# Two MLPs' up-projection in another order, sums of weight blocks given out later, a recurrence's head started later

## The chip, the cores and the metric

One of the eight cores of a Trainium2 chip runs the program. TensorE (PE) multiplies, VectorE (DVE), ScalarE (ACT) and GpSimd (POOL) do the elementwise work, SyncE (SP) issues the loads. The metric is the device time of one execution in microseconds, as the median of several runs.

## The reference

The program is one inference step of a small trunk: a layer with a gated linear recurrence and an MLP, then a layer with dilated windowed attention and an MLP. There are 1024 positions of a prompt and 32 of samples, 1056 columns in all; the width is 1024, the MLPs' hidden width 4096, all in fp32. What the change touches most is the MLP:

```python
def _sqrelu_mlp(x, w_up, w_down):
    return jnp.square(jax.nn.relu(x @ w_up)) @ w_down
...
x = x + _sqrelu_mlp(_rmsnorm(x, mlp_norm[layer]), mlp_w_up[layer], mlp_w_down[layer]).astype(x.dtype)
```

The change also shifts the start of the recurrence's first head. There the state of each of eight heads, 128 x 128, follows S_t = diag(f_t) S_(t-1) + k_t v_t^T, o_t = S_t^T q_t, in chunks.

## The kernel before

Activations lie transposed, features on the partitions and columns along the row. Each fp32 product is three passes of TensorE over a split into a high and a low part: high by high, high by low, low by high (lines L190 to L192 in `mm3`, L986 to L988 in `mmx`). So everything that is multiplied is first split: ScalarE copies the high part, and POOL or VectorE subtracts it from the value to get the low one. For weights that is `_prep` (L131 for `whi` on ScalarE, L132 for `wlo` on POOL, after a load into `wraw`, of which there are few buffers); for hidden values it is `split` in `mlp` (L768 and L769).

The columns fall into three chunks, 384 and 384 and 288. On the first two chunks the MLP uses a scheme of seven products in place of eight for 2 x 2 blocks. It needs sums of blocks of the weights, `wsum` (L159 to L161 on VectorE, L162 on POOL), which are split like weights into `whix` and `wlox`, and combinations of the right operands (L773 and L780 in `combine`). The third chunk is multiplied plainly (`third`, `alone`).

Hidden rows come in eight groups in each MLP. `unit(g, i)`, two for a group, makes 2 x 128 hidden rows: the first half of the inner dimension K by the seven products, whose intermediate sums go through tiles `t` (copies L813 on ScalarE, adds L817 on VectorE); then the rest of K by four plain blocks, `plain(e, c)`, for row block e and chunk c, each of which also takes the relu, the scale and the square and splits the result: (0,0) is entry 0 of the hidden operand `hb`, (1,0) entry 1, (1,1), the corner, entry 2; entries 3 to 6 are combinations. Of chunk 0 POOL makes the low part, otherwise VectorE. L817 and L838 or L834 are the evacuation on VectorE, L839 the square on ScalarE. Of the third chunk the two halves of K are `third(e, 0)` and `third(e, 1)`.

After the two units of a group (but the last), `down` turns the group's hidden rows into four pairs of outputs and adds them to the residual `xr` (L1008; L216 for the third chunk). Its products use `hb` by index: first 0, second 1, third 5, fourth 4, then 6, 3 and 2. Here "down 0" is the first pair of a group, "dn0" to "dn3" are the weights of the four pairs, and "uA" and "uB" those of the units.

A scheduler sets each engine's order from the order in which the code issues the work, with `high_priority` sections moved ahead. `wahead` and `wtake` give out the loads, splits and sums of the next weights; `tick` drives generators that run beside the main work, the late norm (`norm_late`, L311 the scale, L325 the sum over partitions on TensorE) and the recurrence's heads (`gla`; L519 its transposes of `vT`) among them.

Of the kernel before, what the change touches and what calls it, by code (L numbers as in the profile page):

```python
# [28 lines left out]
PW = 384  # L29
# [17 lines left out]
class Kern:  # L47
    def __init__(self, nc, tc, aps, ctx):
        self.nc, self.tc, self.a, self.ctx = nc, tc, aps, ctx
        self.const = ctx.enter_context(tc.tile_pool(name="const", bufs=1))  # L50
        self.op = [self.const.tile([P, KD, NT], F32R, name=n) for n in ("opH", "opL")]
        self.chunks = CHUNKS
        self.wp = ctx.enter_context(tc.tile_pool(name="wp", bufs=2))
        self.pp = ctx.enter_context(tc.tile_pool(name="pp", bufs=4, space=PSUM))
        self.pg = ctx.enter_context(tc.tile_pool(name="pg", bufs=4, space=PSUM))
        self.wx = None
        self.wt = {}
        self.wi = 0
        self.wq = self.weight_order()
        self.queue, self.lanes = deque(), []  # L60
        self.merged = 0
        self.every, self.ticks = 0, 0
        self.rawx = False
        self.twos = False
        self.fine = False
# [59 lines left out]
    def _prep(self, i):  # L125
# [8 lines left out]
        with self.tc.high_priority(offset=400 if i > 1 else 0):  # L134
# [15 lines left out]
            self.wt[i] = (hi, lo)  # L150
        if two:
            with self.tc.high_priority(offset=20):

# [10 lines left out]
                pair(sh, sl, 4, u)  # L164
                self.wt[i] = (hi, lo), (sh, sl)

# [166 lines left out]
    def phase_a(self):  # L333
# [144 lines left out]
        self.open_scales()  # L478
        self.lanes.append(self.norm_late(G_M0, ops, NEED, hp=100))
        next(self.lanes[-1])  # L480
# [103 lines left out]
    def gla(self, h, b, kt, q, vT, og):  # L584

        nc, gp, a = self.nc, self.gp, self.a
        vt = gp.tile([P, 8, P], F32, name="vt8", bufs=1)
        for i in range(2):
# [163 lines left out]
    def mlp(self, layer, ops, after=None):  # L752
# [46 lines left out]
        def unit(g, i):  # L799
# [98 lines left out]
            if not first:  # L898
                W1 = self.wtake()
                self.wahead(self.wi)  # L900
                order = [lambda: third(0, 1), lambda: third(1, 1)]
                rest = [lambda: plain(1, 0, "c"), lambda: plain(0, 0, "a")]
                for f in rest[::-1] if last else order + rest:
                    yield
                    f()
                yield
                bank[1, 1] = self.bank()[:, :PW]
                plain(1, 1, "b", True)
                yield
            else:  # L910
# [8 lines left out]
                split(h[2], x)  # L919
            plain(0, 1)  # L920
            if not last:
                h = rows()
                combine(t, lambda k, v: split(h[k], v))
            if last:
                for f in order:
                    yield
                    f()

# [6 lines left out]
        for g in range(NG):  # L935
# [4 lines left out]
            B = [hb[i][1] for i in range(2)]  # L940
            W = self.wtake()
            self.wahead(self.wi)
            for i in range(2):
                self.alone(0, i, W, hs)
                self.tick()
            for p in range(4):
                if p < 3:
                    nxt = []

                    def fill(i):  # L950
                        if not nxt:
                            nxt.append(self.wtake())
                        self.alone(2 * p + 2, i, nxt[0], hs)
                        self.tick()
                else:
                    u = unit(g + 1, 0)
                    fill = lambda i: next(u)
                self.down(2 * p, W, B, fill)
                self.tick()
                if p < 3:  # L960
                    W = nxt[0]
                    self.wahead(self.wi)
        self.sctx.close()
        w = [self.wnext() for _ in range(4)]
# [79 lines left out]
    def phase_c(self, ops):  # L1044
# [56 lines left out]
        self.open_scales()  # L1101
        self.lanes.append(self.norm_late(G_M1, ops, NEED))
        next(self.lanes[-1])
# [558 lines left out]
```

## Time and profile before

| | |
|---|---|
| median of 3 runs | 3006.82 us (3006.81 to 3012.26) |
| profiled execution | 3012.01 us, its span 3010.2 us |
| TensorE busy | 2856.8 us, 95% of the span |
| VectorE busy | 1832.2 us, 61% |
| ScalarE busy | 1426.9 us, 47% |
| GpSimd busy | 1374.9 us, 46% |
| mean granted clock of TensorE | 0.988 of full speed |

The engine's waits and the timeline of one group are the places to read: what each of TensorE's pauses waited for, how often it comes, and what the engine named was doing just then. Windows show the clock that was granted in a stretch: the share that is missing from it, times the stretch's length, is the time lost.

### The profile page before, as it was taken

Reading aid. Unit: us, or ns where it says so; the run is one execution under the profiler, and the core shown is the slowest. Engines: PE = TensorE matmul, PEld = TensorE weight load, DVE = VectorE, ACT = ScalarE, POOL = GpSimd, SP = SyncE. Lnnn points to the kernel's source line nnn. Section 1 sums busy time; section 2 is a strip of 40 time slices with the busy share of each in tenths; the row PEclk is TensorE's granted clock in tenths of the full one; section 3 lists DMA queues with packets and bytes.
Section 4 is the critical chain, followed back from the end, with each engine's and each line's share of the span. In section 5 each row is a group of like instructions: output and inputs, shape, how many; then the busy total and the mean of one; then the engine's idle time right before and its main releaser. Section 6 shows DMA issues by size and latency. Waiting matters only on the chain.

```text
span 3010.2 us, 47500 instructions
## 1 busy us (share of the span) xinstructions
PE 2856.8 (95%) x17952; PEld 2725.9 (91%) x17952; DVE 1832.2 (61%) x3661; ACT 1426.9 (47%) x3233; POOL 1374.9 (46%) x1159
## 2 busy tenths in 40 slices
PE   6999999899999999999999999999998999999999
PEld 5999899899999999999889889889888999999999
DVE  8777777956555545554755555565686555655553
ACT  6677667745333333333445545555555333333332
POOL 5454444534455445454554454343115545445452
PEclk9999999999999999999999999999999999999999
DMA  3111210221111111112212234332631111111112
GB/s 114 37 32 35 73 39 30 86 100 35 43 50 43 43 50 43 50 43 76 92 48 71 75 103 116 125 113 77 218 119 46 47 49 44 47 45 46 46 50 86
DMA packets 131957, 201.91 MB, mean 67 GB/s; under 512 B 26320, under 2 KB 65872, under 8 KB 129680
## 3 DMA queue, kind: packets, MB, share of 16 engines
q1 hardware_dynamic: 131728, 198.88, 21.1%
q8 instruction: 141, 2.31, 0.3%
q14 instruction: 88, 0.72, 0.1%
HBM read 164.04 MB, written 34.80 MB: 66 GB/s over the span
## 4 chain that ended last, share of the span: by engine, by line
PE 54%; DVE 12%; POOL 9%; DMA 7%; issue 5%; ACT 4%; POOLq 0%; DVEq 0%; SPq 0%; ACTq 0%
PE pj L190 7%; PE pj L191 6%; PE pj L192 6%; POOL wlo L132 6%; PE pj L986 6%; PE pj L987 6%; PE pj L988 6%; DMA wraw<-w_dn 4%; PE g L986 3%; PE g L987 3%; PE g L988 3%; PE g L1333 2%; DMA wraw<-w_uA 2%; PE g L1305 2%; DVE tmp L838 1%
## 5 line engine op out<-in xcount | busy, mean ns | idle before, releaser
L132 POOL TENSOR_TENSOR wlo<-wraw,whi 128x512 fp32r<-128x512 f32 x404 | 535.5, 1345 | 715.8 <-ACT whi L131 684.4
L190 PE MATMUL pj<-opH,whi 128*128 128x352 f32 (+2 forms) x1872 | 637.8, 341 | 4.9 <-ACT opH L237 3.5
L191 PE MATMUL pj<-opL,whi 128*128 128x352 f32 (+2 forms) x1872 | 611.7, 327 | 1.5 <-POOL opL L238 1.2
L192 PE MATMUL pj<-opH,wlo 128*128 128x352 f32 (+2 forms) x1872 | 609.8, 326 | 2.7 <-POOL wlo L132 2.7
L131 ACT ACTIVATE whi<-wraw 128x512 fp32r<-128x512 f32 x404 | 232.7, 621 | 360.8 <-PE pj L987 248.6
L190 PEld LDWEIGHTS pj<-opH,whi 128*128 128x128 f32 x1872 | 357.1, 191 | 23.5 <-issue 12.8
L191 PEld LDWEIGHTS pj<-opL,whi 128*128 128x128 f32 x1872 | 358.2, 191 | 11.6 <-issue 5.7
L192 PEld LDWEIGHTS pj<-opH,wlo 128*128 128x128 f32 x1872 | 356.3, 190 | 6.5 <-POOL wlo L132 3.5
L1008 DVE TENSOR_TENSOR xr<-xr,pj 128x384 f32<-128x384 f32 x336 | 181.4, 549 | 134.2 <-PE pj L988 133.1
L132 POOL TENSOR_TENSOR wlox<-wsum,whix 128x512 fp32r<-128x512 f32 x176 | 231.5, 1336 | 44.4 <-ACT whix L131 44.4
L162 POOL TENSOR_TENSOR wsum<-wraw,wsum 128x256 f32<-128x256 f32 x88 | 68.5, 778 | 358.3 <-DVE wsum L160 239.0
L131 ACT ACTIVATE whix<-wsum 128x512 fp32r<-128x512 f32 x176 | 106.6, 628 | 190.9 <-PE pj L987 69.7
L986 PE MATMUL g<-opH,whi 128*128 128x288 f32 (+1 forms) x640 | 195.1, 305 | 0.0
L987 PE MATMUL g<-opL,whi 128*128 128x288 f32 (+1 forms) x640 | 194.6, 304 | 0.0
L988 PE MATMUL g<-opH,wlo 128*128 128x288 f32 (+1 forms) x640 | 194.1, 303 | 0.0
L986 PE MATMUL pj<-opH,whi 128*128 128x384 f32 x512 | 174.9, 342 | 3.4 <-ACT whi L131 3.4
L988 PE MATMUL pj<-opH,wlo 128*128 128x384 f32 x512 | 173.8, 339 | 1.5 <-POOL wlo L132 1.5
L987 PE MATMUL pj<-opL,whi 128*128 128x384 f32 x512 | 173.7, 339 | 0.0
L544 POOL TENSOR_TENSOR lv<-b 128x512 f32<-128x512 f32 x112 | 125.1, 1128 | 104.3 <-PE g L645 56.7
L159 DVE TENSOR_TENSOR wsum<-wraw 128x256 f32<-128x256 f32 x88 | 46.2, 525 | 142.1 <-DMA wraw<-w_dn 73.7
L986 PEld LDWEIGHTS g<-opH,whi 128*128 128x128 f32 x640 | 120.7, 189 | 0.0
L988 PEld LDWEIGHTS g<-opH,wlo 128*128 128x128 f32 x640 | 120.5, 188 | 0.0
(431 smaller groups left out, 7648.2 us busy)
## 6 DMA issues: line engine op xcount, KB each, us to landing
wraw<-w_dn SPq DMA_DIRECT2D x128, 256.0 KB, 2.9
wraw<-w_in SPq DMA_DIRECT2D x64, 256.0 KB, 2.8
wraw<-w_uA SPq DMA_DIRECT2D x64, 256.0 KB, 2.9
wraw<-w_uB SPq DMA_DIRECT2D x64, 256.0 KB, 2.9
wraw<-w_q SPq DMA_DIRECT2D x48, 256.0 KB, 3.0
ub<-us SPq DMA_DIRECT2D x32, 256.0 KB, 2.2
cc<-ck SPq DMA_DIRECT2D x8, 1024.0 KB, 4.9
cc<-cv SPq DMA_DIRECT2D x8, 1024.0 KB, 5.1
```

What stands on the lines that cost most here:

```text
L131: nc.scalar.activation(hi[:, j:j + 4, :], raw, AF.Copy)
L132: nc.gpsimd.tensor_tensor(lo[:, j:j + 4, :], raw, hi[:, j:j + 4, :].bitcast(F32), op=ALU.subtract)
L162: nc.gpsimd.tensor_tensor(u[:, 2:], a12, t[:, 2:], op=ALU.subtract)
L190: nc.tensor.matmul(ps, wh[:, kw, :], xh[:, kx, :], start=(i == 0), stop=False)
L191: nc.tensor.matmul(ps, wh[:, kw, :], xl[:, kx, :], start=False, stop=False)
L192: nc.tensor.matmul(ps, wl[:, kw, :], xh[:, kx, :], start=False, stop=(i == len(ks) - 1))
L544: nc.gpsimd.tensor_tensor(r(lv), r(b), r(b)[:, :, h - 1:h].to_broadcast([P, 256 // h, 2 * h]), op=ALU.subtract)
L986: nc.tensor.matmul(ps, wh[:, kw, :], xh, start=start and i == 0, stop=False, skip_group_check=True)
L987: nc.tensor.matmul(ps, wh[:, kw, :], xl, start=False, stop=False, skip_group_check=True)
L988: nc.tensor.matmul(ps, wl[:, kw, :], xh, start=False, stop=stop and i == len(items) - 1, skip_group_check=True)
L1008: self.nc.vector.tensor_tensor(x(i, c), x(i, c), ps, op=ALU.add)
L1305: nc.tensor.matmul(out[r], qs[r][:, j * P:(j + 1) * P], k, start=True, stop=True)
```

## The change

Four parts. (a) In the groups with a `down`, the sums of the next weights are not given out with the load and the split but are kept in `sumq` and given out by `flush`, in the fill of the next pair of outputs. (b) In all units but the first and those of the last group, the rest of K goes in the order (0,0), corner, (0,1), (1,0), after the third chunk's two; it was (1,0), (0,0), corner, (0,1). (c) The first head of the recurrence yields two steps before it starts. (d) `norm_late` takes three more steps ahead of the last of its gaps, in both MLPs. No instruction is added or taken away.

```diff
@@ _prep
         if two:
+            box = []
+            self.wt[i] = (hi, lo), box
+
+            def sums():
+                box.extend(self.sums(raws, pair))
+            if self.late:
+                self.sumq.append(sums)
+            else:
+                sums()
+
+    def flush(self):
+        while self.sumq:
+            self.sumq.pop()()
+
+    def sums(self, raws, pair):
+        nc = self.nc
+        if True:
             with self.tc.high_priority(offset=20):
...
-                self.wt[i] = (hi, lo), (sh, sl)
+                return sh, sl
@@ the norms ahead of the MLPs
-        self.lanes.append(self.norm_late(G_M0, ops, NEED, hp=100))
+        self.lanes.append(self.norm_late(G_M0, ops, NEED, (3, 3, 5), 100))
...
-        self.lanes.append(self.norm_late(G_M1, ops, NEED))
+        self.lanes.append(self.norm_late(G_M1, ops, NEED, (3, 3, 5)))
@@ gla
+        if h == 0:
+
+            yield from (None,) * 2
@@ unit
+                def corner():
+                    bank[1, 1] = self.bank()[:, :PW]
+                    plain(1, 1, "b", True)
                 order = [lambda: third(0, 1), lambda: third(1, 1)]
-                rest = [lambda: plain(1, 0, "c"), lambda: plain(0, 0, "a")]
-                for f in rest[::-1] if last else order + rest:
+                rest = [lambda: plain(0, 0, "a"), corner, lambda: plain(0, 1), lambda: plain(1, 0, "c")]
+                if last:
+                    rest = [rest[0], rest[3], rest[1], rest[2]]
+                for f in rest + order if last else order + rest:
                     yield
                     f()
-                yield
-                bank[1, 1] = self.bank()[:, :PW]
-                plain(1, 1, "b", True)
-                yield
...
-            plain(0, 1)
+                plain(0, 1)
@@ mlp
             W = self.wtake()
+            self.late = True
             self.wahead(self.wi)
...
                         self.alone(2 * p + 2, i, nxt[0], hs)
+                        self.flush()
                         self.tick()
                 else:
                     u = unit(g + 1, 0)
-                    fill = lambda i: next(u)
+
+                    def fill(i):
+                        next(u)
+                        self.flush()
...
+            self.late = False
```

In the kernel after, lines shift: L131 is L132 there, L132 is L133, L159 to L162 are L177 to L180, L216 is L234, L519 is L537, L768 and L769 are L789 and L790, L773 and L780 are L794 and L801, L817 is L838, L834 is L855, L838 and L839 are L859 and L860.

VectorE, the end of unit 1 of a group in the first MLP, from dn1's sums (`wsum`) on. `tmp_11245` is the tile of (1,0), `tmp_11212` that of (0,0), `tmp_11237` the corner, `tmp_11414` that of (0,1). Before:

```order
L159 TENSOR_TENSOR wsum_11441<-wraw_11435 128x256
L161 TENSOR_TENSOR wsum_11442<-wraw_11431,wraw_11435 128x256
L160 TENSOR_TENSOR wsum_11441<-wsum_11441,wraw_11431 128x256
L769 TENSOR_TENSOR hs1L_11327<-g_11273,hs1H_11326 128x288
L817 TENSOR_TENSOR tmp_11245<-tmp_11245,pj_11230 128x384
L838 SCALAR_TENSOR_TENSOR tmp_11245<-tmp_11245,scale0_6816 128x384
L817 TENSOR_TENSOR tmp_11212<-tmp_11212,pj_11205 128x384
L838 SCALAR_TENSOR_TENSOR tmp_11212<-tmp_11212,scale0_6816 128x384
L817 TENSOR_TENSOR tmp_11237<-tmp_11237,g_11384 128x384
L838 SCALAR_TENSOR_TENSOR tmp_11237<-tmp_11237,scale1_6817 128x384
L834 SCALAR_TENSOR_TENSOR tmp_11414<-pj_11204,scale1_6817 128x384
L769 TENSOR_TENSOR hb1L_11329<-tmp_11237,hb1H_11328 128x384
```

After, from the row behind the three sums of dn1 on, which stand at the same place; (0,1) is `tmp_11397` here:

```order
L790 TENSOR_TENSOR hs1L_11327<-g_11273,hs1H_11326 128x288
L838 TENSOR_TENSOR tmp_11212<-tmp_11212,pj_11205 128x384
L859 SCALAR_TENSOR_TENSOR tmp_11212<-tmp_11212,scale0_6816 128x384
L838 TENSOR_TENSOR tmp_11237<-tmp_11237,g_11367 128x384
L859 SCALAR_TENSOR_TENSOR tmp_11237<-tmp_11237,scale1_6817 128x384
L855 SCALAR_TENSOR_TENSOR tmp_11397<-pj_11204,scale1_6817 128x384
L790 TENSOR_TENSOR hb1L_11329<-tmp_11237,hb1H_11328 128x384
L794 TENSOR_TENSOR tmp_11212<-tmp_11397,tmp_11212 128x384
L794 TENSOR_TENSOR tmp_11397<-tmp_11237,tmp_11397 128x384
L838 TENSOR_TENSOR tmp_11245<-tmp_11245,pj_11230 128x384
L790 TENSOR_TENSOR hb1L_11329<-tmp_11212,hb1H_11328 128x384
L859 SCALAR_TENSOR_TENSOR tmp_11245<-tmp_11245,scale0_6816 128x384
```

The add and the multiply of (1,0) (`tmp_11245`) moved from the head of the row behind the other three blocks; the add now stands behind two L794, and the multiply behind one more split, in the last row shown.

POOL, the same place, from the split of dn1's sums on; `wlo_11430` is the low part of dn1 itself. Before:

```order
L132 TENSOR_TENSOR wlox_11440<-wsum_11441,whix_11439 128x512
L132 TENSOR_TENSOR wlox_11440<-wsum_11442,whix_11439 128x512
L769 TENSOR_TENSOR hb1L_11329<-tmp_11245,hb1H_11328 128x384
L769 TENSOR_TENSOR hb1L_11329<-tmp_11212,hb1H_11328 128x384
L132 TENSOR_TENSOR wlo_11430<-wraw_11431,whi_11429 128x512
L132 TENSOR_TENSOR wlo_11430<-wraw_11435,whi_11429 128x512
```

After:

```order
L133 TENSOR_TENSOR wlox_11513<-wsum_11514,whix_11512 128x512
L133 TENSOR_TENSOR wlox_11513<-wsum_11515,whix_11512 128x512
L790 TENSOR_TENSOR hb1L_11329<-tmp_11212,hb1H_11328 128x384
L133 TENSOR_TENSOR wlo_11430<-wraw_11431,whi_11429 128x512
L133 TENSOR_TENSOR wlo_11430<-wraw_11435,whi_11429 128x512
L790 TENSOR_TENSOR hb1L_11329<-tmp_11245,hb1H_11328 128x384
```

The low part of (1,0) (from `tmp_11245`) moved from ahead of dn1's two `wlo` to behind them.

ScalarE, the same place, from the square of (1,0) before and of (0,0) after. Before:

```order
L839 ACTIVATE tmp_11245<-tmp_11245 128x384
L768 ACTIVATE hb1H_11328<-tmp_11245 128x384
L839 ACTIVATE tmp_11212<-tmp_11212 128x384
L768 ACTIVATE hb1H_11328<-tmp_11212 128x384
L839 ACTIVATE tmp_11237<-tmp_11237 128x384
L768 ACTIVATE hb1H_11328<-tmp_11237 128x384
L131 ACTIVATE whi_11429<-wraw_11431 128x512
L131 ACTIVATE whi_11429<-wraw_11435 128x512
L839 ACTIVATE tmp_11414<-tmp_11414 128x384
```

After:

```order
L860 ACTIVATE tmp_11212<-tmp_11212 128x384
L789 ACTIVATE hb1H_11328<-tmp_11212 128x384
L860 ACTIVATE tmp_11237<-tmp_11237 128x384
L789 ACTIVATE hb1H_11328<-tmp_11237 128x384
L860 ACTIVATE tmp_11397<-tmp_11397 128x384
L789 ACTIVATE hb1H_11328<-tmp_11212 128x384
L132 ACTIVATE whi_11429<-wraw_11431 128x512
L132 ACTIVATE whi_11429<-wraw_11435 128x512
L789 ACTIVATE hb1H_11328<-tmp_11397 128x384
L860 ACTIVATE tmp_11245<-tmp_11245 128x384
L789 ACTIVATE hb1H_11328<-tmp_11212 128x384
L789 ACTIVATE hb1H_11328<-tmp_11245 128x384 x2
```

The square of (1,0) and its high part moved from ahead of dn1's two `whi` to behind them and behind two combinations' high parts.

TensorE, the transposes of the recurrence's first head among the products of the input projection. Before:

```order
L192 MATMUL pj_657<-opH_58,wlo_547 128x352
L519 MATMUL g_671<-ident_126,vT_545 128x128 x4
L519 MATMUL g_677<-ident_126,vT_545 128x128 x4
L190 MATMUL pj_657<-opH_58,whi_546 128x352
L191 MATMUL pj_657<-opL_59,whi_546 128x352
```

After:

```order
L208 MATMUL pj_683<-opH_58,whi_546 128x352
L209 MATMUL pj_683<-opL_59,whi_546 128x352
L210 MATMUL pj_683<-opH_58,wlo_547 128x352
L537 MATMUL g_697<-ident_126,vT_545 128x128 x4
L537 MATMUL g_703<-ident_126,vT_545 128x128 x4
L208 MATMUL pj_683<-opH_58,whi_546 128x352
```

They moved 24 matmuls of 352 columns further on.

## Rows read from the trace of the kernel before

**Rows 1.** The page: the span, and TensorE's busy time, share and instructions.

```profile
span 3010.2 us, 47500 instructions
...
PE 2856.8 (95%) x17952; PEld 2725.9 (91%) x17952; DVE 1832.2 (61%) x3661; ACT 1426.9 (47%) x3233; POOL 1374.9 (46%) x1159
```

**Rows 2.** TensorE's waits: line, what it waited for, us in total, times, longest.

```profile
PE pj L986 <- DVE xr L1008: 26.9, 42, 1.2
...
PE pj L986 <- ACT hb1H L768: 12.4, 14, 2.0
...
PE pj L986 <- DVE tmp L817: 11.5, 13, 1.1
...
PE g L519 <- ACT vT L377: 5.1, 2, 3.7
...
PE pj L987 <- DVE hb1L L769: 4.4, 14, 0.4
```

**Rows 3.** TensorE's timeline, one group: start, us, operation [idle before, releaser].

```profile
1119.32 0.45 PE L986 MATMUL pj<-opH,whix 128*128 128x384 f32 x1 [0.95 <-DVE tmp L817]
...
1136.86 0.33 PE L986 MATMUL g<-hb1H,whi 128*128 128x384 f32 x1
...
1137.03 0.33 PE L987 MATMUL g<-hb1L,whi 128*128 128x384 f32 x1
...
1138.86 0.45 PE L986 MATMUL pj<-hb1H,whix 128*128 128x384 f32 x1 [0.80 <-ACT hb1H L768]
...
1140.54 0.44 PE L986 MATMUL pj<-hb0H,whix 128*128 128x384 f32 x1 [0.32 <-DVE xr L1008]
```

**Rows 4.** VectorE's timeline, the same group.

```profile
1126.74 0.42 DVE L159 TENSOR_TENSOR wsum<-wraw 128x256 f32<-128x256 f32 x1 [2.25 <-DMA wraw<-w_dn]
...
1128.70 1.69 DVE L838 SCALAR_TENSOR_TENSOR tmp<-tmp,scale 128x384 f32<-128x384 f32 x1
...
1130.89 1.07 DVE L838 SCALAR_TENSOR_TENSOR tmp<-tmp,scale 128x384 f32<-128x384 f32 x1
...
1133.18 0.54 DVE L834 SCALAR_TENSOR_TENSOR tmp<-pj,scale 128x384 f32<-128x384 f32 x1
...
1135.93 2.32 DVE L773 TENSOR_TENSOR tmp<-tmp 128x384 f32<-128x384 f32 x2 [0.60 <-ACT tmp L839]
```

**Rows 5.** Timelines of ScalarE and POOL, the same group.

```profile
1133.85 0.53 ACT L768 ACTIVATE hb1H<-tmp 128x384 fp32r<-128x384 f32 x1
...
1134.28 1.14 ACT L131 ACTIVATE whi<-wraw 128x512 fp32r<-128x512 f32 x2
...
1121.15 2.52 POOL L132 TENSOR_TENSOR wlo<-wraw,whi 128x512 fp32r<-128x512 f32 x2
...
1133.16 1.02 POOL L769 TENSOR_TENSOR hb1L<-tmp,hb1H 128x384 fp32r<-128x384 f32 x1 [0.32 <-ACT hb1H L768]
...
1134.97 2.86 POOL L132 TENSOR_TENSOR wlo<-wraw,whi 128x512 fp32r<-128x512 f32 x2 [0.79 <-ACT whi L131]
```

**Rows 6.** TensorE's timeline at three long waits elsewhere.

```profile
318.17 1.20 PE L562 MATMUL g<-lv,lk 128*128 128x128 f32 x4 [3.14 <-DVE st L726]
...
711.40 1.33 PE L325 MATMUL g<-scale,onesD 128*128 128x288 f32 x2 [3.90 <-DVE scale L311]
...
2265.94 0.44 PE L986 MATMUL pj<-opH,whi 128*128 128x384 f32 x1 [3.42 <-ACT whi L131]
```

**Rows 7.** TensorE by windows: us, busy (count), granted clock, DMA share, GB/s.

```profile
66.00:80.00 14.00, 8.94 (x46) 0.76 0.12 37
...
316.00:322.00 6.00, 3.83 (x17) 0.72 0.43 140
...
768.00:772.00 4.00, 4.00 (x19) 0.57 0.02 4
...
2266.00:2274.00 8.00, 6.48 (x22) 0.57 0.22 70
...
2600.00:2606.00 6.00, 5.69 (x26) 0.72 0.04 14
```

More of the change, by code (lines that the diff above doesn't have):

```diff
@@ L57, in __init__ @@
         self.wt = {}
+        self.late, self.sumq = False, []
         self.wi = 0
@@ L923, in unit @@
                 combine(t, lambda k, v: split(h[k], v))
[L924 to L927, printed above, removed]
         def run(u):
```

## The prediction

> **What bounds the kernel now.** I read the page first: TensorE is busy for 95% of the span of 3010.2 us [rows 1], so a change that adds or removes no instruction can only move the time by TensorE's waits and by its clock. The list of TensorE's waits comes next [rows 2]. Its repeating entries belong to the MLPs and come 14 times each, once in each of the seven groups with a `down` in two MLPs (the residual's L1008 three times): the residual add L1008 (26.9 us, 42 times), the ScalarE part of a split, L768 (12.4), the add L817 (11.5), the VectorE part of a split, L769 (4.4). Those are the waits that the new order can touch; the wait for `vT` (5.1 us, of which 3.7 in one) is the one that the recurrence's edit can touch.
>
> The timeline of one group shows where they stand [rows 3]. Unit 1 waits 0.95 us for L817 at 1119.32. At the first pair of outputs, down 0, the second product meets its operands without a wait (1136.86 and 1137.03, 0.17 apart: the pitch of a full-speed matmul), and the third product, which wants the combination (index 5), waits 0.80 at 1138.86, then 0.31 for its low part [rows 2]; the fourth begins at 1140.54 after 0.32. The reader should see that the second product, hidden entry 1 = (1,0), is on time today only because `plain(1,0)` is the first of the four plain blocks.
>
> **The VectorE queue, part (a).** The sums of the next weights are given out later in the code, but the order built from it has dn1's three at the same row of VectorE's queue, ahead of the last `hs1L` split, before as after; those of the two later pairs and of the next unit also stay but for places of one or two rows, and the loads' order on SP is the same. So L159 still waits 2.25 us for the load of dn1 at 1126.74 and everything behind it in VectorE's queue waits with it [rows 4]; the load itself hangs on POOL's `wlo` of dn0, which ends at 1121.15 + 2.52 and which nothing moves [rows 5]. Cost of (a): nothing, and no gain; the two L1008 waits of the later downs remain. L1008 at down 0 has one more sum ahead of it at most (0.42), beneath the longer wait found below.
>
> **The order of the rest of K, part (b).** It takes the last use of L817's tile out of the way, so that the 0.95 wait goes, with about 0.3 of refill: TensorE asks for (1,0) at down 0 about 1.25 us earlier, at 1136.86 − 1.25 = 1135.6. But (1,0) is now the last of the four blocks. Its chain, on the clock of [rows 3 to 5]:
> VectorE: the part from the first L817 to L834 loses one add and one multiply. From 1128.1 (one L817 ahead of the L838 at 1128.70), with L838 at 1.69 and 1.07 (both run beside POOL), L817 at 0.54 twice and L834 at 0.54, it ends near 1132.4, where it now ends at 1133.7. Then `h2L` behind ScalarE's three steps at 0.53 [rows 5], to 1133.6; two L773 to 1134.6; L817 of (1,0) to 1135.1; `h3L` to 1135.6; and only then L838 of (1,0).
> ScalarE: `h3` to 1134.7, the two `whi` of dn1, 1.14, to 1135.8; then `h5`, square of (1,0), `h4`, `h1`.
> POOL: the `wlo` of dn1, 2.86 for the two, starts 0.69 after `whi` starts, as now, so 1135.4 to 1138.2; behind it, in order, the low part of (1,0), 1.02.
> What L838 and the next L773 take beside POOL is the doubtful term. The two L773 that ran beside `wlo` took 2.32 instead of 1.0 [rows 4]. If L838 comes in ahead of POOL, L838 ends at 1136.2, L773 near 1137.9, `h4` 1138.4, `h1` 1138.9, low part 1140.0. If POOL is ahead, the two end 1137.2 and 1138.7, `h4` 1139.2, `h1` 1139.8, low part 1140.8 to 1141.0.
> From the low part on there are eight matmuls of 0.17 and a refill of 0.1 to the fourth product: it begins at 1141.5 to 1142.4 in place of 1140.54, so +1.0 to +1.9 a group; the waits of 0.80, 0.31 and 0.32 are gone by then, since their operands come meanwhile, and are counted in this difference. A floor, if ScalarE's `h1` were ready when POOL's `wlo` ends (1137.9 + 1.02): the fourth product at 1140.4, −0.1. I take **+1.5 × 14 = +21 us**, nearest to the pair of L773 rows, with −1.4 to +29 as ends.
> One rule is weighed here. The rows show POOL's two-piece `wlo` at 2.52 with VectorE idle and 2.86 with two L773 beside it, so 0.17 more for each [rows 5]. The Trainium skill ("SBUF — State Buffer", section "SBUF: two separate sides") says that VectorE operations with two SBUF inputs and GpSimd's operations take one port pair as a lock for the whole instruction, and the loser fully blocks. By it POOL too would stand still for each whole VectorE operation, about 0.5 for each in place of 0.17, the low part would land some 0.6 later, +2.1 a group, and the sum would be +29 instead of +21. It speaks against this change; the trace bears out VectorE's side of it and not POOL's.
>
> **TensorE's clock.** The new wait at the second product is 1138.9 (or 1139.8) less 1135.6, so 3.3 to 4.2 us, and about 0.9 more for the low part. What such a wait costs afterwards is read from the trace by length of stretch times what is missing from the clock. After a wait of 3.14 [rows 6] the clock was 0.72 over 6 us, a loss of 1.7; after 3.42 it was 0.57 over 8 us, a loss of 3.4 [rows 7]. That is TensorE at 1.2 GHz instead of 2.4 for 3.4 and 6.9 us. Today five of the 14 downs 0 have such a stretch of 1.7 (the first at 768, the last at 2600 [rows 7]). With 2.5 for each of 14, less 5 × 1.7: **+26.5 us**; ends 0 (as now) and 14 × 3.4 − 8.5 = +39.
>
> **The recurrence's first head, part (c).** Two steps later, its first transposes stand 24 matmuls of 352 columns further on; at under 0.17 each those are up to 3.9 us of TensorE's work laid over 5.1 us of waits for `vT` [rows 2], and the slow stretch 66 to 80 lost 14 × 0.24 = 3.4 us [rows 7], of which I count half. The head's first transposes move with everything that they issue; head 1's come 12 matmuls later, those of head 2 and on stand where they stood. **−5 us**, ends −8 and −2.
>
> **The late norm, part (d).** L325 for the last chunk moves behind three further blocks of the first unit and so loses its wait of 3.90 at 711.40 [rows 6], but TensorE would then wait for the second weight's `whi`, which comes at the same time (in the second MLP the 3.42 at 2265.94 is that wait by name [rows 6]). No gain there; behind it the scale of chunk 2 stands later on ScalarE, worth up to 1.5 us for the copies in each MLP. **+1**, ends −4 and +4.
>
> **Sum.** On the profiled execution's 3012.0 us: +21 + 26.5 − 5 + 1 = +43.5, so 3055.5. That execution was 5.2 above the median of the three runs, 3006.8; on the median it gives 3050.
>
> **Rivals.**
> Rival A, the wait is short and the clock holds: `h1` comes before POOL is free, each group stays where it was (−0.1 × 14 = −1.4) and no new slow stretch comes: 3006.8 − 1.4 − 5 + 1 = 3001. For it: five waits of 1.4 in sum already bring slow stretches and nine such do not, so length alone doesn't decide. Against it: VectorE's queue behind 1126.74 is full to the end of the chain.
> Rival B, faster: the chain is ready before TensorE wants it. It decides at 1135.6: were the low part of (1,0) done by then, 4.5 to 5.3 us sooner than worked out, all the waits in unit 1 and down 0 would go: 0.95 + 0.80 + 0.31 + 0.32 and four refills of 0.27, 3.4 a group, × 14 = −48; the five slow stretches, −8.5; −5 for the head, +1: 2946. That needs the sums not to hold VectorE at 1126.74, so dn1's load some 2.25 us sooner, and ScalarE and POOL to take (1,0) ahead of dn1's split. For it: that is where the code gives the sums out. Against: the queues as built show neither.
> That part (a) does not do what it says is thus part of the forecast.
>
> **Chances and range.** Forecast 0.60; A 0.20 (within 0.2% 0.12, slower 0.05, faster 0.03); B 0.15; something still slower, as a later down that falls behind in each group, 0.05. What a measurement of this kernel can tell from no change is about 0.2%, 6 us. Faster 0.18, same 0.12, slower 0.70. The range holds the forecast's ends and A and leaves out B and the tail: the upper end is +29 + 39 − 2 + 4 = +70, 3077, the lower reaches below A to 2985, for a chain that gains a little in each group.
>
> **What would show it.** In the profile after: the L817 entry gone from TensorE's waits; a new entry at L986 in `g<-hb1H` for L789 (L768 before) with 14 times 3 us or more, and one for POOL's L790 in L987; the third product without its 0.80; L177 still waiting for its load ahead of the chain; more half-clock stretches after the downs 0; two waits for `vT` in sum below 2 us. I am wrong if the second product waits less than 2 us, if POOL has (1,0) ahead of `wlo`, or if the clock stays at full speed after the new wait.

## The result, and the profile after

The changed kernel takes 3049.2 us (median of four runs, 3047.13 to 3051.89) against 3006.82: the ratio is 1.0138 with a 95% interval of 1.0121 to 1.0156. It is slower by 42 us, where 3050 was predicted. The profiled execution took 3051.89 us, its span is 3050.1.

The page of the changed kernel, its span and busy times (to set beside [rows 1]):

```profile
span 3050.1 us, 47505 instructions
...
PE 2873.4 (94%) x17952; PEld 2748.4 (90%) x17952; DVE 1856.2 (61%) x3661; ACT 1420.4 (47%) x3233; POOL 1374.2 (45%) x1159
```

TensorE is busy for 16.6 us more, though it has the same instructions: they took longer. The other part of the 39.9 us more of span is idle time. TensorE's waits in the changed kernel (line, what it waited for, us in total, times, longest):

```profile
PE g L1010 <- ACT hb1H L789: 48.4, 14, 5.2
...
PE pj L1010 <- DVE xr L1032: 22.9, 28, 1.7
...
PE pj L1010 <- ACT whi L132: 9.0, 2, 4.6
...
PE g L1011 <- POOL hb1L L790: 7.8, 14, 0.7
```

Beside [rows 2]: the waits for L817's add (L838 now) are gone but for 0.3 us; the two of the third product are gone; in their place stand one for the high part of (1,0), 14 times, 3.5 us on average (2.75 to 5.21), and one for its low part, 14 times 0.55. The residual adds' 42 waits became 28, those of the second and third pair; those did not change (22.8 us before, 22.9 now). The row of `whi` is the start of the two MLPs, where TensorE waits for a unit's second weight.

The timeline of TensorE in the same group as [rows 3], which now runs about 8 us later, and the same place one group on:

```profile
1148.02 0.69 PE L1010 MATMUL g<-hb1H,whi 128*128 128x384 f32 x1 [3.38 <-ACT hb1H L789]
...
1149.21 0.69 PE L1011 MATMUL g<-hb1L,whi 128*128 128x384 f32 x1 [0.50 <-POOL hb1L L790]
...
1150.01 0.52 PE L1010 MATMUL pj<-hb0H,whix 128*128 128x384 f32 x1
...
1150.33 0.52 PE L1011 MATMUL pj<-hb0L,whix 128*128 128x384 f32 x1
...
1243.27 0.69 PE L1010 MATMUL g<-hb1H,whi 128*128 128x384 f32 x1 [3.13 <-ACT hb1H L789]
```

The second product begins after 3.38 us, loses 0.50 more for the low part, and then goes on at a pitch of 0.32 instead of 0.17. The place comes round after 95.3 us (1148.02 to 1243.27). In the kernel before, the same matmul came round after 91.9 (1136.86 to 1228.80).

VectorE's timeline ahead of that, beside [rows 4]:

```profile
1134.98 0.42 DVE L177 TENSOR_TENSOR wsum<-wraw 128x256 f32<-128x256 f32 x1 [2.86 <-DMA wraw<-w_dn]
...
1136.94 1.67 DVE L859 SCALAR_TENSOR_TENSOR tmp<-tmp,scale 128x384 f32<-128x384 f32 x1
...
1141.82 1.15 DVE L794 TENSOR_TENSOR tmp<-tmp 128x384 f32<-128x384 f32 x2
...
1143.83 1.63 DVE L859 SCALAR_TENSOR_TENSOR tmp<-tmp,scale 128x384 f32<-128x384 f32 x1
...
1145.38 1.62 DVE L794 TENSOR_TENSOR tmp<-tmp 128x384 f32<-128x384 f32 x1
```

The reader should see the chain in the order in which it was worked out: the first sum waits 2.86 for dn1's load; the multiply of (0,0) takes 1.67 beside POOL; two L794 (the L773 of before) come ahead of (1,0); then the multiply of (1,0) and the next combination take 1.63 and 1.62, while GpSimd makes `wlo`. ScalarE at that place, beside [rows 5]:

```profile
1142.85 1.14 ACT L132 ACTIVATE whi<-wraw 128x512 fp32r<-128x512 f32 x2
...
1147.03 0.94 ACT L789 ACTIVATE hb1H<-tmp 128x384 fp32r<-128x384 f32 x2 [1.02 <-DVE tmp L794]
```

The second of the two in the last row is the high part of (1,0). And POOL, its first row the split of dn0, the next two the halves of dn1's split:

```profile
1129.40 2.54 POOL L133 TENSOR_TENSOR wlo<-wraw,whi 128x512 fp32r<-128x512 f32 x2
...
1143.54 1.50 POOL L133 TENSOR_TENSOR wlo<-wraw,whi 128x512 fp32r<-128x512 f32 x1 [2.47 <-ACT whi L132]
...
1145.01 1.58 POOL L133 TENSOR_TENSOR wlo<-wraw,whi 128x512 fp32r<-128x512 f32 x1
...
1148.04 1.11 POOL L790 TENSOR_TENSOR hb1L<-tmp,hb1H 128x384 fp32r<-128x384 f32 x1 [1.46 <-ACT hb1H L789]
```

The two `whi` of dn1, the two `wlo` of dn1 and only then the low part of (1,0), which ends at 1149.15. GpSimd is free from 1146.58 on and waits 1.46 for the high part, which in its turn waits for VectorE. TensorE by windows (us, busy, count, granted clock, DMA share, GB/s), through that place and over the first MLP:

```profile
1146.00:1147.00 1.00, 0.00 (x0) 1.00 0.72 164
...
1147.00:1148.00 1.00, 0.00 (x0) 0.64 0.36 119
...
1148.00:1149.00 1.00, 0.69 (x1) 0.50 0.65 223
...
1154.00:1155.00 1.00, 1.00 (x9) 0.95 0.00 0
...
702.00:1476.00 774.00, 726.29 (x4355) 0.96 0.16 49
```

and the same stretch of the kernel before:

```profile
702.00:1476.00 774.00, 735.68 (x4454) 0.98 0.17 51
```

TensorE is idle from 1144.64. Its clock is full until 1147, falls to 0.50, that is 1.2 GHz, inside the next microsecond, while TensorE still waits, stays there through six microseconds of matmuls and is back to full speed just behind 1154. Over the first MLP the clock is 0.96, in the kernel before it was 0.98. A stretch at 0.50 is called a slow stretch below. At the 14 first pairs the change has eleven of 6.8 us and three of 3.4; the kernel before has five of 3.4 there. How many there are varies from one execution to the next: the two kernels below in which the groups keep the old order on all engines (the old order of the rest of K, the head alone) have three and two.

### The profile page after: what moved, and what is told of

Same layout as the page of the kernel before. It is cut to its first block, busy times and chain, and to the rows that moved or that the text cites. A ratio compares the mean times of both kernels' runs of the same rounds, so it can differ in the third digit from the quotient of the medians.

```text
span 3050.1 us, 47505 instructions
## 1 busy us (share of the span) xinstructions
PE 2873.4 (94%) x17952; PEld 2748.4 (90%) x17952; DVE 1856.2 (61%) x3661; ACT 1420.4 (47%) x3233; POOL 1374.2 (45%) x1159
## 5 line engine op out<-in xcount | busy, mean ns | idle before, releaser
L133 POOL TENSOR_TENSOR wlo<-wraw,whi 128x512 fp32r<-128x512 f32 x404 | 540.0, 1356 | 850.2 <-ACT whi L132 809.1
L132 ACT ACTIVATE whi<-wraw 128x512 fp32r<-128x512 f32 x404 | 232.8, 621 | 402.0 <-PE pj L1011 284.0
L133 POOL TENSOR_TENSOR wlox<-wsum,whix 128x512 fp32r<-128x512 f32 x176 | 229.8, 1327 | 47.1 <-ACT whix L132 47.1
L132 ACT ACTIVATE whix<-wsum 128x512 fp32r<-128x512 f32 x176 | 106.7, 629 | 202.1 <-DVE wsum L178 85.4
L180 POOL TENSOR_TENSOR wsum<-wraw,wsum 128x256 f32<-128x256 f32 x88 | 66.1, 751 | 260.9 <-DVE wsum L178 166.8
L177 DVE TENSOR_TENSOR wsum<-wraw 128x256 f32<-128x256 f32 x88 | 49.0, 557 | 134.5 <-DMA wraw<-w_dn 68.8
```

The lines of the kernel that those rows point to most:

```text
L132: nc.scalar.activation(hi[:, j:j + 4, :], raw, AF.Copy)
L133: nc.gpsimd.tensor_tensor(lo[:, j:j + 4, :], raw, hi[:, j:j + 4, :].bitcast(F32), op=ALU.subtract)
L177: tt(t[:, :2], a21, a22, op=ALU.add)
L180: nc.gpsimd.tensor_tensor(u[:, 2:], a12, t[:, 2:], op=ALU.subtract)
```

## The experiments

All kernels ran beside the kernel before; the ratios are to it, with their 95% intervals. (1,0) is `plain(1, 0)`, dn1 the weights of a group's second pair.

| kernel | median us | ratio | interval |
|---|---|---|---|
| the change | 3049.2 | 1.0138 | 1.0121 to 1.0156 |
| old order of the rest of K | 3007.1 | 0.9984 | 0.9975 to 0.9994 |
| new order in unit 1 alone | 3054.7 | 1.0142 | 1.0120 to 1.0164 |
| new order in unit 0 alone | 3011.2 | 1.0007 | 0.9996 to 1.0018 |
| the change, late sums on GpSimd | 3035.3 | 1.0086 | 1.0070 to 1.0103 |
| the change, wait filled with 18 matmuls | 3026.0 | 1.0049 | 1.0027 to 1.0071 |
| the change without dn1's sums | 2985.5 | 0.9917 | 0.9895 to 0.9938 |
| old order, later sums on GpSimd | 2983.9 | 0.9910 | 0.9885 to 0.9935 |
| the same, mixed order, a block moved | 2981.4 | 0.9906 | 0.9884 to 0.9928 |
| the change, dn1's sums behind the chain | 3013.9 | 1.0012 | 0.9997 to 1.0027 |
| mixed order, all sums out of the way | 2932.3 | 0.9734 | 0.9710 to 0.9757 |
| old order, all sums out of the way | 2942.5 | 0.9772 | 0.9751 to 0.9793 |
| the head alone | 3005.8 | 0.9979 | 0.9967 to 0.9990 |

### Which part costs the time

Theory: part (b), because (1,0) comes last and its chain stands behind dn1's load and split. Rivals: the sums given out later, or the norm. The first kernel takes part (b) back and keeps the rest.

```diff
                 if last:
                     rest = [rest[0], rest[3], rest[1], rest[2]]
+                else:
+                    rest = [rest[k] for k in (3, 0, 1, 2)]
```

> The changed kernel with the old order of the rest of K; the later sums, the head two steps later and the later norm stay. Theory (the place of block (1,0) makes the time): the groups come back to a period of 92 us, the wait for hb1H at the second product is gone, and what is left are the head's about -3 and the norm's about +2: 3001 to 3010 us. Rival (the sums given out later, or the norm, cost the time): it stays above 3030.

```profile
PE pj L1012 <- DVE xr L1034: 26.3, 41, 1.1
...
PE pj L1012 <- ACT hb1H L789: 12.5, 14, 1.3
...
PE pj L1012 <- DVE tmp L838: 11.5, 13, 1.1
```

The three waits are those of [rows 2], in size and number, and the time is 3007.1. So part (b) makes the whole loss, and the three other parts together bring a gain of 0.16% (0.06 to 0.25). With part (a) alone the queues of VectorE, ScalarE, GpSimd and TensorE as built are those of the kernel before, row for row, so that kernel was not run. The traces bear it out: the run with the old order and the run with the head alone, which differ by (a) and the norm, have the same instructions in the same order on all four engines, but for some rows of the norm at the start of the two MLPs. So (a) moves nothing by itself.

### Do the waits of a group add up?

The new order in one of the two units tells whether TensorE is late by the sum of its waits, or by the end of a chain that starts elsewhere. The first kernel has the new order in unit 1 alone; the second has `i == 1` in this line, and so the new order in unit 0 alone.

```diff
                 if last:
                     rest = [rest[0], rest[3], rest[1], rest[2]]
+                elif i == 0:
+                    rest = [rest[k] for k in (3, 0, 1, 2)]
```

> The changed kernel with the new order of the rest of K in unit 1 of a group alone, the old one in unit 0. Theory (the second product of the first pair waits for a chain that starts at dn1's load, so what comes before it in unit 1 doesn't matter): unit 1's wait for L838's add comes back with about 0.9 in each group, the wait at the second product falls by as much, from 3.4 to about 2.2, and the time is that of the changed kernel, 3040 to 3053. Rival (waits add up): the add's 1.25 in each group comes on top, 14 x 1.25 = 17.5: about 3066.

> The changed kernel with the new order of the rest of K in unit 0 alone, the old one in unit 1. Theory (chain from dn1's load): unit 1's wait for the add is gone, but the third product of the first pair waits as much longer, 0.8 to about 2.0, so nothing is gained against the old order in both: 3000 to 3010. Rival (waits add up): the 1.25 in each group is gained, 2986 to 2992, the third product's wait stays at 0.8.

TensorE's waits with the new order in unit 1 alone:

```profile
PE g L1012 <- ACT hb1H L789: 40.4, 14, 3.2
...
PE pj L1012 <- DVE tmp L838: 12.4, 13, 1.1
...
PE g L1013 <- POOL hb1L L790: 10.0, 14, 0.8
```

and in unit 0 alone:

```profile
PE pj L1012 <- ACT hb1H L789: 19.0, 14, 1.7
...
PE pj L1012 <- DVE tmp L838: 0.2, 1, 0.2
```

In the first, unit 1's wait for the add is back with 12.4 us, and the wait for the high part has fallen from 48.4 to 40.4, that for the low part risen from 7.8 to 10.0: the sum is larger by some 6 us and the time the same within the intervals (1.0142 against 1.0138). The clock gave back about as much: of the 14 slow stretches at the first pairs only two are long here, eleven in the change. In the second the add's 11.5 us are gone, the third product waits for 19.0 instead of 12.5, and the time is that of the old order or a little above (1.0007 against 0.9984). The times are those of the theory and not of its rival, though both medians lie just above the expected ranges, by 1.7 and 1.2 us. The single waits bear it out only in part: the second product's wait fell by 0.6 a group and not by 0.9 or more. By size the third product's wait rose by half a microsecond, not by 1.2, and the gain of the rest did not show in the time: in its profiled execution the second kernel has eight slow stretches at the 14 first pairs, the one with the old order three, about 10 us more of lost clock. That this took the gain back is argued from one execution of each, not shown.

### Where the chain hangs

If VectorE's queue is late because its first sum waits for dn1's load, the sums must be taken off that queue. The first try moves all late sums to GpSimd.

```diff
-                tt = nc.vector.tensor_tensor
+                tt = (nc.gpsimd if self.late else nc.vector).tensor_tensor
```

> The changed kernel, with the sums of the groups' dn1, dn2, dn3 and the next unit's weights on GpSimd in place of VectorE (three more instructions there for each). Theory (VectorE stands with the whole chain of (1,0) behind the first sum, which waits for dn1's load): VectorE goes on without the load, the high part of (1,0) is ready before TensorE wants it, the wait of 3.4 goes, that for the low part (GpSimd takes it behind dn1's own low part, 1.2 later than now in its queue but no longer behind VectorE) is at most 0.8, and the residual adds' waits (22.9 us), which stand behind the other sums, fall: 2960 to 3005. Rival (GpSimd is the bound, or the queue that waits for the load merely changes): the second product still waits over 2 us, 3035 or more.

```profile
PE g L1010 <- ACT hb1H L789: 62.2, 14, 5.7
```

ScalarE's timeline in the same group of that kernel, and VectorE's:

```profile
1133.40 0.63 ACT L132 ACTIVATE whix<-wsum 128x512 fp32r<-128x512 f32 x1 [4.78 <-POOL wsum L178]
```

```profile
1134.37 0.46 DVE L790 TENSOR_TENSOR hs1L<-g,hs1H 128x288 fp32r<-128x288 f32 x1 [6.17 <-ACT hs1H L789]
```

The expectation missed: the second product waits longer, 4.4 us. The row on ScalarE shows why. `whix` of dn1's sums stands there ahead of the high part of unit 1's third chunk (`hs1H`), and waits 4.78 us for the sum on GpSimd, which waits for the load; VectorE then stands 6.17 us behind `hs1H`. The wait had moved from one in-order queue to another and reached VectorE all the same, behind three sums that take 0.74 each on GpSimd and 0.42 on VectorE. The residual adds' 22.9 us are gone, and the second product's longer wait takes 14 of them back. That leaves 9 of the 14 us that this kernel gains on the change; the rest no run took apart. The rival was right on the chain, the theory on the adds.

So the next kernel takes dn1's sums out altogether; the second pair uses the first pair's.

```diff
-        if two:
+        if two and self.reuse:
+            self.wt[i] = (hi, lo), self.reuse
+        elif two:
...
+            self.reuse = W[1]
             self.wahead(self.wi)
+            self.reuse = None
```

> The changed kernel without the sums of dn1 and their split: the second pair of each group uses the first pair's sums in their place, so the output is not the reference's. dn1's load and its own split stay where they are. Theory (the chain of (1,0) stands in VectorE's and ScalarE's queues behind the sums that wait for dn1's load): the chain starts some 3 us earlier, the wait of 3.4 for the high part goes, that for the low part behind dn1's split stays under 1, the half clock after the first pair too, and so do most of the 40 us: 2985 to 3012. Rival (the order on ScalarE and POOL behind dn1's own split, and VectorE beside POOL, set the chain): a wait of over 2 us stays at the second product, 3030 or more.

```profile
PE g L1016 <- POOL hb1L L793: 10.5, 14, 0.8
...
PE g L1015 <- ACT hb1H L792: 9.5, 14, 1.0
```

The wait for the high part fell from 48.4 to 9.5 us, that for the low part stayed at 10.5, and no slow stretch is left at the first pairs. The time is 2985.5, at the lower end of what was expected; a part of that is the work left out. The remaining 0.7 and 0.75 a group are put down to dn1's own split, beside which two operations of the chain still take 1.65 each on VectorE, and to GpSimd's 1.11 for the low part; no run took these away.

Nothing is left out in the next: dn1's first sum is multiplied by a one that VectorE makes from the last combination, so that it can't stand ahead of the chain.

```diff
-                tt(t[:, :2], a21, a22, op=ALU.add)
+                if self.gate is None:
+                    tt(t[:, :2], a21, a22, op=ALU.add)
+                else:
+                    nc.vector.scalar_tensor_tensor(t[:, :2], a21, self.gate, a22, op0=ALU.mult, op1=ALU.add)
+                    self.gate = None
...
+                if i == 1:
+                    self.gate = hp.tile([P, 1], F32, name="gate")
+                    nc.vector.tensor_scalar(self.gate, t[1, 0][:, :1], 0.0, 1.0, op0=ALU.mult, op1=ALU.add)
```

> The changed kernel, with dn1's first sum multiplied by a one that VectorE makes from the end of the chain of combinations: so the sums of dn1 stand behind the chain in VectorE's queue, which the change's code asks for and its queues don't show. Nothing is left out. Theory (the chain of (1,0) is late because it stands behind the sums that wait for dn1's load): the waits at the second product fall as without dn1's sums, to about 0.7 and 0.75, the half clock there goes, and the time is 2985 to 3005. Rival (dn1's sums then come late themselves): new waits at the second pair's third product for whix or wlox, 3010 or more.

```profile
PE pj L1018 <- DVE xr L1040: 46.9, 28, 2.6
...
PE g L1019 <- POOL hb1L L795: 10.5, 14, 0.8
...
PE g L1018 <- ACT hb1H L794: 9.2, 14, 0.7
```

The second product's waits are those of the run without the sums, 9.2 and 10.5, so the mechanism holds. The time is 9 to 29 us above what was expected: the residual adds now wait 46.9 us instead of 22.9, and the whole rise is the second pair's, 34.4 us instead of 11.0. VectorE's timeline in one group of that kernel shows the next sum, of dn2, ahead of a residual add:

```profile
1145.01 0.43 DVE L179 TENSOR_TENSOR wsum<-wraw 128x256 f32<-128x256 f32 x1 [2.48 <-POOL wlo L134]
```

It waits 2.48 us for the second half of dn2's load, which landed at 1144.92; GpSimd's `wlo`, which the row names, happened to end in the same moment. dn1's raw block is now read last by GpSimd's sum from 1140.44 to 1141.18, behind its own split; the second half of dn2's load was issued at 1141.21, right behind it, and the adds of the second pair pay for that. The rival expected new waits at the second pair's third product; they stand at the adds.

### What the clock costs

The windows show half a clock after the new wait. To tell the clock's share from the wait's, matmuls are laid into the wait.

```diff
-                self.down(2 * p, W, B, fill)
+                self.down(2 * p, W, B, fill, 3 if p == 0 else 0)
...
+        for _ in range(pad):
+            prod(C, w, 0, 0, True, True)
         prod(C, w, 2, 1, True, True)
```

> The changed kernel with 18 more matmuls of 384 columns in each group, ahead of the second product of the first pair, into its own bank, which the product then starts anew: 18 x 0.175 = 3.15 us of work laid into the wait of 3.4 us. What is disputed is how much of the loss of 2.9 us a group is the wait and how much is TensorE's half clock after it. Theory (the half clock follows the wait, and about 1.7 of the 2.9 us is the clock's): the wait falls to under 0.5, the clock stays at full speed at these places, and the kernel gets faster for all its added work: 3018 to 3032. Rival (the clock's share is small and the wait all): same time within 0.2%, 3043 to 3055, or slower.

TensorE's waits at the second product:

```profile
PE g L1011 <- POOL hb1L L790: 10.4, 14, 0.7
...
PE g L1010 <- ACT hb1H L789: 3.8, 12, 0.7
```

and TensorE's window over the first MLP, columns as above:

```profile
702.00:1476.00 774.00, 743.52 (x4548) 0.99 0.17 51
```

The kernel does 252 matmuls more and is faster by 23 us by the medians, 27 by the ratios. The wait for the high part fell to 3.8 us in all, the granted clock of the first MLP is 0.99, and the slow stretches at the 14 first pairs are gone. So somewhat over half of the loss is put down to the clock: 23 to 27 of 42 to 46 us. That figure is a balance of two larger ones. TensorE's busy time in slow stretches, counted at the half that is missing from the clock, comes to 58 us in the trace of the change and to 25 here, so 33 were given back, some of them from stretches that the kernel before has as well; the added matmuls cost 8, since they take 46 us and the idle time fell by 38.

### Versions that beat both

With the old order the second and third pair's waits remain. Their sums, not dn1's, go to GpSimd:

```diff
-                tt = nc.vector.tensor_tensor
+                tt = (nc.gpsimd if onpool else nc.vector).tensor_tensor
...
             self.late = True
             self.wahead(self.wi)
+            self.onpool = True
```

> The old order of the rest of K, and the sums of dn2, dn3 and the next unit on GpSimd; dn1's stay on VectorE. Theory (the residual adds of the second and third pair wait because VectorE's queue stands at the next sums, which wait for their loads): 28 waits of 0.78 with a refill of 0.27 each go, about -29 us against the old order: 2972 to 2985. Rival (GpSimd's split comes later by the sums' 2.2 us and TensorE waits for weights instead): 2998 or more, with new waits for wlo or wlox.

```profile
PE pj L1015 <- DVE tmp L840: 12.1, 14, 1.1
...
PE pj L1015 <- ACT hb1H L791: 11.9, 14, 1.4
...
PE pj L1016 <- DVE hb1L L792: 6.5, 19, 0.5
...
PE pj L1015 <- DVE xr L1037: 4.4, 14, 0.3
```

The residual adds' waits fell from 26.3 to 4.4 us, and the time is 2983.9, as expected. Then the mixed order, new in unit 0 and old in unit 1, and one block of the third chunk moved between the first pair's second and third product:

```diff
+            def between():
+                self.alone(0, 1, W, hs)
                 self.tick()
...
         prod(C, w, 2, 1, True, True)
+        if between:
+            between()
         prod(B, s, 4, 5, True)
```

> The new order in unit 0, the old one in unit 1, the sums as in the run with the old order and GpSimd's sums, and one of the two third-chunk blocks ahead of the first pair moved between its second and third product, 12 matmuls, 1.6 us. Theory: unit 1's wait for L838's add is gone (new order in unit 0), and the third product's chain, which cannot start earlier than dn1's load, gets 1.6 us more: its waits of 1.36, 0.3 and 0.3 shrink to under 0.5 in sum, and the second and third pair's waits are gone: 2940 to 2970. Rival (the chain from dn1's load is still late, or the first product now waits for (0,0)): 2972 or more.

```profile
PE pj L1019 <- DVE hb1L L792: 15.0, 28, 0.9
...
PE pj L1018 <- ACT hb1H L791: 12.2, 15, 0.9
```

2981.4, the same as the one ahead of it within the intervals: the rival held. The waits for the add went (12.1), and as many came for low parts, VectorE's (15.0 instead of 6.5) and GpSimd's (4.1). VectorE's first sum still waits for dn1's load:

```profile
1109.39 0.43 DVE L179 TENSOR_TENSOR wsum<-wraw 128x256 f32<-128x256 f32 x1 [2.81 <-DMA wraw<-w_dn]
```

With the load's wait out of the chain (the `gate` of above, sums of dn2 and on at GpSimd) that should be different:

> The new order in unit 0 and the old one in unit 1, dn1's sums behind the chain, the sums of dn2, dn3 and the next unit on GpSimd. Theory: against the old order with GpSimd's sums, unit 1's wait for L840's add (0.95 and a refill of 0.27) goes, and the third product's 0.85 and 0.3 shrink since the chain no longer stands behind dn1's load: 14 x 1.2 to 14 x 2.7 less than 2984, so 2946 to 2967. Rival (dn1's sums late for the second pair, or the chain bound by ScalarE and GpSimd as it was): 2975 or more.

> The same with the old order in both units. Theory: unit 1's wait for the add stays, since it comes from unit 0's tail, and the third product's waits shrink: 2955 to 2980, above the run with the new order in unit 0 by 10 to 17. Rival (the two units' orders don't add up, as they did not while the chain stood behind the load): the same as that run within 5 us.

TensorE's waits in the groups, mixed order:

```profile
PE pj L1023 <- DVE xr L1045: 2.7, 14, 0.2
...
PE pj L1023 <- DVE tmp L845: 0.5, 2, 0.3
```

and old order:

```profile
PE pj L1023 <- DVE tmp L845: 11.7, 14, 1.1
```

2932.3 and 2942.5, better than expected by 14 and 12 us at least: all of the third product's waits are gone, and no slow stretch is left at the first pairs. Of the mixed order's 52 us against the old order with GpSimd's sums (2983.9), 32 are waits (12.1, 11.9, 6.5 and 4.4 us there, 2.7 and 0.5 here), up to 12 are seven slow stretches at first pairs, with 1.7 lost in each; the rest is put down to the refill behind 14 times four waits (the matmuls before and behind a wait no longer overlap, which the prediction counts at about 0.3), and no run took it apart. Now the unit's order counts: the two differ by 10 us, as expected, about the add's wait of 11.7 against 0.5. That is the point of the mixed order, and it did not show as long as both ended at the load (3011.2 against 3007.1 above). The mixed order with all sums out of the way is 2.7% faster than the kernel before (0.9734, 0.9710 to 0.9757).

### The head alone

The kernel before, with the two lines of `gla` from the change and nothing else:

> The kernel before with the first head two steps later and nothing else. Theory: the waits for vT go from 5.1 to under 2 us, the slow stretch from 70 to 80 us goes too, and the rest stays: 3 to 5 us faster, a ratio of 0.9983 to 0.999. Rival (the recurrence's later heads give it back): no difference, 0.9995 to 1.0005.

```profile
PE g L537 <- ACT vT L395: 1.3, 1, 1.3
```

5.1 us of waits became 1.3, and the ratio is 0.9979 (0.9967 to 0.9990): 3 to 10 us, the expectation's 3 to 5 among them.

## Why the prediction was right

**What bounds the kernel.** Right: no instruction was added, and the time moved by waits and clock alone. The places named were the places.

**Part (a).** Right: dn1's sum stands where it stood and waits for the load, 2.86 (2.25 in [rows 4]). The cost of nothing, gain of nothing follows from equal queues and from the old-order run and its trace, not from a run of (a) alone. The 28 waits of the later pairs stayed.

**Part (b).** The wait was given as 3.3 to 4.2 for the high part and about 0.9 for the low one; measured are 3.5 and 0.55 on average. L838 (L859 now) and the next combination took 1.63 and 1.62, which is the branch with POOL ahead; the low part, worked out at 1140.8 to 1141.0, ended at 1149.15, and with dn1's first sum 8.24 later than in [rows 4] that is 1140.9. The step that the run without the sums and the one with `gate` bear out is the anchor, dn1's load; the run with the sums on GpSimd adds that it binds through ScalarE's queue as well, which the prediction had not seen.

**The rule on the port pair.** In sum GpSimd's two halves of `wlo` took 3.04 here and 2.54 at dn0. Shared out over the two long VectorE operations, as the prediction did with [rows 5], that is 0.25 for each, as against 0.17 there and about 0.5 by the rule of the Trainium skill ("SBUF — State Buffer", section "SBUF: two separate sides"). But sharing it out is a wrong reading, here and in the prediction. The multiply ended 0.42 behind the first half, the combination 0.42 behind the second and last: the combination was held by GpSimd, and nothing shows that it slowed it. By halves, GpSimd took 1.50 beside the end of a low part on VectorE and 1.58 beside the end of the multiply, where a half takes 1.30 at dn0. In the kernel before, where only the first of the two L773 was still running when the second half began, the halves took 1.29 and 1.60. So each VectorE operation that GpSimd ran into cost it 0.2 to 0.3, and the prediction's "VectorE's side of it and not POOL's" goes too far: the trace shows a wait on both sides, as the rule has it, but for GpSimd a shorter one than the whole VectorE operation of about 0.5. That the sum by rows came out, 1140.9 and not some 0.6 later, is so in spite of that reading.

**The clock.** +26.5 was right in size, but the way there has a flaw. The length of a slow stretch times the clock that is missing counts time in which TensorE waits anyway: at 1148 the stretch begins some 0.7 us ahead of the matmul, and the 0.50 for the low part lie in it too, so 0.6 of its 3.4 cost nothing. By length the loss at the first pairs is 3.4 in each of 11 long stretches and 1.7 in each of three short ones, less 1.7 in each of the five of before: 34 us more. Counting only the time in which TensorE works, a long stretch cost 1.9 to 3.0, 2.7 on average, and the loss grew by 26 (34 less the 8.5 of before). The estimate came out because it took 2.5 for every stretch, between the two sizes that the rows had; most were long and cost a little more, three were short. That the mean came so near is in part luck, the more so as the number of slow stretches in the kernel before varies between executions. The 23 to 27 us of the filled wait are near it by a different balance, 33 given back for 8 of work.

**The sum.** The terms for (b) were 21 + 26.5 = 47.5; measured against the old-order run it is 42 by the medians and 46 by the ratios. The clock's 26 leave some 16 to 20 for the waits, where +21 was put; the two traces bear that out, with 23 us more idle time and, the half clock taken off, 8 us less for the same matmuls, which fits 24 waits fewer, each with its refill. The head was put at −5 and measures −6 (−3 to −10) alone. The norm was put at +1; together with the head and the sums it leaves −5 (−2 to −8), so nothing that can be told from that. L325's wait of 3.90 went to the second weight's `whi`, 9.0 us in two waits in the place of 3.4 in one, as the prediction had it.

**The rivals.** A fell: the wait was long, 3.5, and the clock did not hold. B fell. Its condition was that the sums do not hold VectorE ahead of the chain, and the `gate` kernel makes just that true: the loss at the first pair is then gone, but the time is 3013.9 and not B's 2946, since the second pair's adds then wait and 0.7 and 0.75 a group stay at the second product.

## What to carry to other kernels

A block whose result is wanted early must be followed through every in-order queue on its way: what counted here was not where it stands in the code but which wait for a load stands ahead of it, on any of the engines. As long as such a wait set the end, a better order ahead of it gained nothing; once it was taken away, the same order was worth 10 us. A wait of about 3.5 us in TensorE cost up to 3.0 more in clock, and filling it with spare matmuls showed how much. A slow stretch should be counted by the work done in it and not by its length.

## What the runs showed of the hardware

TensorE's clock fell to 1.2 GHz inside waits of 3.1 to 5.2 us and came back some six microseconds after the work had begun again, at eleven of 14 places; at the other three, with waits of 2.8 to 3.2, it fell 0.8 to 2.5 us after the wait's end, for 3.4 us. 252 added matmuls in those waits kept it at full speed at all 14 places and made the program 23 us faster.

A VectorE operation with two operands in SBUF that came while a GpSimd operation ran ended 0.42 us behind it (1.63 us instead of 0.55); the GpSimd operation that came while one of VectorE's was running took 0.2 to 0.3 us longer (1.50 and 1.58 instead of 1.30).
